# Another opening for a hybrid encoder block: value products in six PSUM banks, adaLN row sums in PSUM, norm sums on TensorE

## The chip, the cores and the metric

The kernel runs on one core of one Trainium2 chip, in one launch. Times are device microseconds of that core, from a profiled execution or from repeated timed runs; for repeated runs the median is given. TensorE (PE) multiplies matrices into PSUM, which has eight banks of 128 x 512 float32; VectorE (DVE), ScalarE (ACT) and GpSimd (POOL) work element by element; SyncE (SP) issues nearly all the DMA transfers.

## What is computed

One encoder block on 1024 positions of width 1024, float32, batch 1, conditioned by a vector `c`. Cut to what matters here:

```python
ada = silu(c) @ w_ada + b_ada                  # 6 x 1024 numbers
shift1, scale1, gate1, shift2, scale2, gate2 = split(ada, 6)
h = rmsnorm(x, g_mix) * (1 + scale1) + shift1
qa, ka, va, qb, kb, vb, ga, gb = split(h @ w_in)      # 8 heads of 64 in each branch; ga, gb are 1024 wide
oa = mixture_of_dilations(qa, ka, va, rel_bias)       # three banded softmaxes, merged by their denominators
ob = neighbourhood_attention_2d(qb, kb, vb, na_rpb)
x += gate1 * ((sigmoid(ga) * (oa @ w_branch_dil) + sigmoid(gb) * (ob @ w_branch_na)) @ w_out)
h2 = rmsnorm(x, g_ffn) * (1 + scale2) + shift2
u_val, u_gate = split(depthwise_conv3(h2 @ w_up))
x += gate2 * ((gelu(u_gate) * u_val) @ w_down)
y = rmsnorm(x, g_final)
```

## The kernel before

Positions lie on the free axis in two halves of 512 (`hf` = 0, 1); the width 1024 is cut into eight slices of 128 (`k`). Every large product is done three times in a reduced float32 format, "hi x hi, hi x lo, lo x hi", from operands split into a rounded part and the rest: `split` (L55, L56) makes the rounded part on ACT (`whi`, or `a`, `b` for value weights) and the rest on POOL (`wlo`). `h[hf, k]` holds such a pair for the modulated input.

The **opening** ends with the value projections written to DRAM. It is written in an order by hand (`tc.manual_schedule`): each engine and SP's DMA queue take their instructions in the order of the code, and what they wait for follows from the data and from the reuse of buffers. It consists of

- the norm: ACT squares `x` (L181), DVE adds the squares of four slices (L183), `norm_sums` sums over partitions on TensorE by one-column matmuls against `ones` (`add_sums`, L89), `rstd_of` (L94 to L96) makes the factor, and four transposes (`bcast`, L102) spread it over a bank `pbc`;
- the adaLN vector: `w_ada` comes in 12 chunks of 512 columns. For each, `ada_rows` multiplies eight rows by the numbers of `silu(c)` and adds them up on DVE in an SBUF tile `mt` (L149 for the first row, L151 for the rest), `ada_sums` sums over partitions on TensorE (L140), a bias is added (L167). The columns of chunks 0 to 3 are permuted so that each gives shift and scale of two slices `k` (`piece_bias`, L215 and L217);
- `modulate`: per slice DVE multiplies `x` by scale and norm into a PSUM tile `st` (L201, two buffers), ACT adds the shift and rounds to hi (L202), DVE makes lo (L204);
- the value products of two branches and two halves: `v_products` (L236 to L238), four banks of 128 positions, eight slices, three matmuls, 384 of 128x512 in all. They go as four sections of 96: branch 0 half 0 (as the pieces of adaLN become ready), branch 1 half 0, branch 0 half 1, branch 1 half 1. `v_out` (L246) copies four banks by ACT and stores them; banks come from a pool of five named `pj`;
- `warm` (L210): matmuls without a use, in front of the first products;
- loads of the first two query/key weights (`w_load`, L60), DRAM copies of the values in other orders (`va_chunks`, L252 and L254; `vb_chunks`, L456).

Behind the opening a scheduler orders the instructions: eight pairs of heads, each with query/key products (`qk_tiles`, which calls `product`, L77 to L79) and attention. A head of branch A takes its biases by DMA (L485, L486), adds `lnm` (loaded at L694) on POOL, and loads its values (`va_load`, L431 to L434); scores and softmax are L497 and L498, the transposes of P L520. Gates, branch products, output, and the ConvFFN follow.

Of the kernel before, what the change touches and what calls it, by code (L numbers as in the profile page):

```python
# [28 lines left out]
def hybrid_encoder(tc, xT, c, w_ada, small, w_in, w_v, p1_bias, p23_bias, na_bias, ln2_mult, ident, w_br, w_out,  # L29
# [101 lines left out]
    def stage():  # L131
        return ps.tile([128, 512], FT, name="st", bufs=2)

    def ada_sums(parts, pa=None, stop=True):

        first = pa is None
        pa = stage() if first else pa
        for i, (w, col) in enumerate(parts):
            for m in range(4):
                pe.matmul(pa[:, m:m + 1], w[:, m * 128:(m + 1) * 128], col, start=first and i + m == 0,  # L140
                          stop=stop and i == len(parts) - 1 and m == 3, skip_group_check=True)
        return pa

    def ada_rows(rows, ts, acc=None):

        for t in ts:
            if acc is None:
                acc = small_tile()
                dve.tensor_scalar(acc, rows[t], cs[:, t:t + 1], None, OP.mult)  # L149
            else:  # L150
                dve.scalar_tensor_tensor(acc, rows[t], cs[:, t:t + 1], acc, OP.mult, OP.add)  # L151
        return acc
# [12 lines left out]
    def ada_bias(c0, pa):  # L165
        cc = slice(c0, c0 + 4)
        dve.tensor_tensor(ada[:, cc], pa[:, :4], b_ada[:, cc], OP.add)  # L167

# [8 lines left out]
    def squares(x, engines):  # L177
        accs = []
        for k in range(KT):
            sq = small_tile()  # L180
            act.activation(sq, x[k], AF.Square)  # L181
            if k % 4:
                engines[k // 4].tensor_tensor(accs[-1], accs[-1], sq, OP.add)  # L183
            else:
                accs.append(sq)
        return accs

    def norm_sums(accs):
        pcol = ps.tile([128, 512], FT, name="pc")
        add_sums(pcol, accs[0], True, False)  # L190
        add_sums(pcol, accs[1], False, True)
        return pcol

    def modulate(x, hf, ks, pb):

        last = ()
        for k in [*ks, None]:
            if k is not None:
                hi, lo = h[hf, k] = h_tile(), h_tile()
                t, b = stage(), ada[:, k:k + 1]  # L200
                dve.scalar_tensor_tensor(t, x[k], am1[:, k:k + 1], pb, OP.mult, OP.mult)  # L201
                act.activation(hi, t, AF.Identity, bias=b)  # L202
            if last:
                dve.scalar_tensor_tensor(*last, OP.add, OP.subtract)  # L204
            last = k is not None and (lo, t, b, f(hi))
# [13 lines left out]
    v_raws = itertools.count()  # L219

    def v_load(br, kp):
        raw = wpool.tile([128, 2, 512], FT, name="wraw") if next(v_raws) % 4 < 2 else \
            early.tile([128, 2, 512], FT, name="vraw", bufs=2)
        sp.dma_start(raw, w_v[br, kp])
        return raw

    def v_split(raw, w, kp):
        for i in range(2):
            split(raw[:, i], w[0][:, 2 * kp + i], w[1][:, 2 * kp + i], pool)

    def v_products(w, hf, k, banks, ts=range(4)):
        hi, lo = w
        for t in ts:
            p = banks[t]
            hhi, hlo = (x[:, t * 128:t * 128 + 128] for x in h[hf, k])
            pe.matmul(p, hhi, hi[:, k], start=k == 0, stop=False, skip_group_check=True)  # L236
            pe.matmul(p, hhi, lo[:, k], start=False, stop=False, skip_group_check=True)
            pe.matmul(p, hlo, hi[:, k], start=False, stop=k == KT - 1, skip_group_check=True)  # L238

    def v_banks():  # L240
        return [ps.tile([128, 512], FT, name="pj", bufs=5) for _ in range(4)]

    def v_out(br, hf, banks):
        for t, p in enumerate(banks):
# [14 lines left out]
    pas = {}  # L259
    with tc.manual_schedule(engines={e.engine for e in (sp, act, dve, pool, pe)}):  # L260
        x = [x_load(0)]
        sp.dma_start(sm, small)
        rows = {0: ada_load(0, "t0")}
        raws = [v_load(0, 0)]
        rows[1] = ada_load(1, "b1")
        raws.append(v_load(0, 1))
        rows[2] = ada_load(2, "b2")
        raws += [v_load(0, kp) for kp in (2, 3)]
        rows[3] = ada_load(3, "t0")
        x.append(x_load(1))  # L270
        vw = [(t16("a0"), t16("a1"))]

        idle = ps.tile([128, 512], FT, name="pj", bufs=5)[:, :128]
# [9 lines left out]
        v_split(raws[0], vw[0], 0)  # L283
        pa = ada_sums([(acc, ones)])
        warm(6)
        banks = v_banks()
        for q in range(4):
            piece_bias(q, pa)
            modulate(x[0], 0, range(2 * q, 2 * q + 2), pb)
            v_products(vw[0], 0, 2 * q, banks)  # L290
            if q < 3:
                v_split(raws[q + 1], vw[0], q + 1)
                acc = ada_rows(rows[q + 1], range(6))
                pa = ada_sums([(rows[q + 1][t], cs[:, t:t + 1]) for t in (6, 7)], stop=False)
            else:
                accs = squares(x[1], (dve, dve))
            v_products(vw[0], 0, 2 * q + 1, banks, (0, 1))
            if q < 3:
                ada_sums([(acc, ones)], pa)
            v_products(vw[0], 0, 2 * q + 1, banks, (2, 3))  # L300
        raws = [v_load(1, kp) for kp in range(4)]
        vw.append((t16("b1"), t16("b2")))
        rows = {4: ada_load(4, "t0"), 5: ada_load(5, None)}
        pcol = norm_sums(accs)
        r = rstd_of(pcol, 4)
        for kp in range(2):
            v_split(raws[kp], vw[1], kp)
        qk_raw = []
        old = (0, 0, banks)
        accs = {}  # L310
        for n in range(24):
            g, k = divmod(n, 8)
            br, hf = ((1, 0), (0, 1), (1, 1))[g]
            if k == 0:
                v_out(*old)
                banks = v_banks()
                old = br, hf, banks
            if n == 17:
                va_chunks(slice(0, 512))
            v_products(vw[br], hf, k, banks)  # L320
            if n == 0:
                pb = bcast(r, ps, "pc")
                for kp in (2, 3):
                    v_split(raws[kp], vw[1], kp)
                modulate(x[1], 1, range(8), pb)
            if n in (5, 6):
                qk_raw.append(w_load(w_in[4 * (n - 5)]))
            i = n // 2 - 2
            if n % 2 == 0 and 0 <= i < 8:
                accs[i] = ada_rows(rows[4 + i], range(KT))  # L330
                if i < 6:
                    rows[6 + i] = ada_load(6 + i, (None, "t0")[i % 2 == 0])
            if n % 2 and n >= 9:
                i = (n - 9) // 2
                ada_bias(4 * (i + 4), ada_sums([(accs[i], ones)]))
            if n == 12:
# [996 lines left out]
```

## Time and profile before

| what | number |
|---|---|
| runs | 1573.51, 1574.42, 1581.34 us, median 1574.42 us |
| the profiled execution's own time | 1572.37 us |
| its span, first to last instruction | 1570.5 us |
| mean granted TensorE clock | 0.982 of full |
| PE busy | 1505.5 us (96%) |
| DVE, ACT, POOL busy | 1035.6, 779.1, 740.6 us |
| first value product, first query/key product | at 22.99 us, at 149.30 us |

In a row of the timeline stand the start, the duration, the engine, the line, the operation, what it writes and reads, and how many instructions the row groups; in square brackets the time for which the engine was idle before it, and what ended that. A matmul of 128x512 lasts longer than the distance to the next, because matmuls overlap: what counts is the distance of starts. A one-column matmul and a warming matmul show as two records each. In a row of windows the start and end come first, then the length, busy time and records of each engine, then the granted clock.

### The profile page before, as it was taken

How to read it: one execution, taken by the hardware profiler on the slowest of the kernel's cores; microseconds unless marked ns; L12 is line 12 of the kernel's file. 1: busy time of each engine (PE TensorE's matmuls, PEld its weight loads, DVE VectorE, ACT ScalarE, POOL GpSimd, SP SyncE). 2: the span in 40 equal slices, each digit the busy share in tenths (PEclk: the TensorE clock that was granted, in tenths of full speed). 3: DMA queues.
4: the chain of work that ended last, by engine and by line, in shares of the span. 5: the costliest groups of instructions: out<-in, count | busy, mean ns of one | idle time of the engine just before them, and what ended most of it. 6: DMA issues, size and time to landing. Idle time of an engine off the chain costs nothing.

```text
span 1570.5 us, 21187 instructions
## 1 busy us (share of the span) xinstructions
PE 1505.5 (96%) x7582; PEld 1267.3 (81%) x7582; DVE 1035.6 (66%) x1873; ACT 779.1 (50%) x1419; POOL 740.6 (47%) x475
## 2 busy tenths in 40 slices
PE   7998899999999999999999888999999999999998
PEld 6787788888888998887778777888888887778777
DVE  7694366576766655535534898776666667877765
ACT  3420466566765766643344454444444446575542
POOL 2310523233324444311145858676666665778621
PEclk8899999999999999999999999999999999999999
DMA  9577632323245565555544212322222224523313
GB/s 374 193 272 282 171 80 93 100 73 107 75 108 144 149 160 139 170 174 172 175 136 141 94 54 81 108 81 81 82 87 87 81 74 144 189 97 122 115 53 108
DMA packets 110001, 205.21 MB, mean 131 GB/s; under 512 B 40356, under 2 KB 55588, under 8 KB 109860
## 3 DMA queue, kind: packets, MB, share of 16 engines
q1 hardware_dynamic: 109624, 203.59, 40.3%
q8 instruction: 60, 0.98, 0.3%
q14 instruction: 45, 0.37, 0.1%
q10 hardware_dynamic: 272, 0.26, 0.1%
HBM read 158.73 MB, written 42.47 MB: 128 GB/s over the span
## 4 chain that ended last, share of the span: by engine, by line
PE 64%; DVE 12%; DMA 8%; POOL 6%; issue 4%; ACT 4%; SPq 1%; DVEq 0%; ACTq 0%; POOLq 0%
PE pj L822 8%; PE pj L823 8%; PE pj L824 8%; PE pj L79 8%; PE pj L77 8%; PE pj L78 8%; DMA g<-gs 2%; DMA wraw<-w_down 2%; PE pj L378 2%; DVE mt L151 2%; DVE big L1018 2%; PE O L672 2%; POOL wsl L56 2%; POOL wlo L56 1%; PE T L660 1%
## 5 line engine op out<-in xcount | busy, mean ns | idle before, releaser
L56 POOL TENSOR_TENSOR wlo<-wraw,whi 128x1024 fp32r<-128x1024 f32 (+1 forms) x77 | 178.9, 2323 | 249.6 <-ACT whi L55 224.4
L79 PE MATMUL pj<-h,wlo 128*128 128x512 f32 x448 | 178.6, 399 | 1.4 <-POOL wlo L56 1.4
L77 PE MATMUL pj<-h,whi 128*128 128x512 f32 x448 | 178.4, 398 | 0.1
L78 PE MATMUL pj<-h,whi 128*128 128x512 f32 x448 | 178.2, 398 | 0.0
L56 POOL TENSOR_TENSOR wsl<-big,wsh 128x1024 fp32r<-128x1024 f32 (+1 forms) x45 | 109.5, 2434 | 48.1 <-ACT wsh L55 48.0
L1018 DVE SCALAR_TENSOR_TENSOR big<-wc,sm,big 128x256 f32<-128x256 f32 (+1 forms) x132 | 116.8, 933 | 17.3 <-ACT big L1012 17.2
L55 ACT ACTIVATE whi<-wraw 128x1024 fp32r<-128x1024 f32 (+1 forms) x79 | 80.7, 1022 | 73.7 <-PE pj L78 30.0
L79 PEld LDWEIGHTS pj<-h,wlo 128*128 128x128 f32 x448 | 84.4, 188 | 16.3 <-POOL wlo L56 1.8
L78 PEld LDWEIGHTS pj<-h,whi 128*128 128x128 f32 x448 | 84.3, 188 | 14.4
L77 PEld LDWEIGHTS pj<-h,whi 128*128 128x128 f32 x448 | 84.4, 188 | 14.2 <-PE pj L79 0.5
L449 POOL TENSOR_TENSOR vv<-vv 96x256 fp32r<-96x256 f32 (+2 forms) x32 | 41.2, 1297 | 102.6 <-ACT vv L448 93.1
L498 ACT ACTIVATE P<-P,st 128x256 f32<-128x256 f32 x128 | 64.3, 503 | 49.6 <-DVE st L497 49.3
L385 POOL TENSOR_SCALAR qb<-qs 128x256 fp32r<-128x256 f32 x32 | 26.4, 851 | 124.0 <-PE S L544 57.9
L497 DVE CUSTOM_DVE_ANT_0 P<-S,bias 128x256 f32<-128x256 f32 x128 | 52.4, 421 | 42.3 <-PE S L544 23.2
L1018 DVE SCALAR_TENSOR_TENSOR big<-pj,sm,big 128x512 f32<-128x512 f32 x132 | 67.9, 565 | 16.1 <-ACT big L1012 16.1
L1012 ACT ACTIVATE big<-wc,sm 128x512 f32<-128x512 f32 x44 | 35.8, 816 | 75.7 <-DVE wc L835 45.3
L56 POOL TENSOR_TENSOR wsl<-wraw,wsh 128x768 fp32r<-128x768 f32 (+1 forms) x23 | 49.9, 2171 | 45.5 <-ACT wsh L55 45.5
L650 POOL TENSOR_SCALAR P<-P,stb 128x288 f32<-128x288 f32 (+1 forms) x32 | 39.9, 1248 | 66.0 <-DVE stb L647 58.8
L55 ACT ACTIVATE wsh<-big 128x1024 fp32r<-128x1024 f32 (+1 forms) x45 | 44.8, 1000 | 37.1 <-POOL big L787 23.6
L1044 ACT ACTIVATE big<-big 128x1024 f32<-128x1024 f32 x22 | 23.3, 1060 | 80.2 <-DVE big L1018 80.2
L503 DVE TENSOR_TENSOR tl<-T,th 128x512 fp32r<-128x512 f32 x64 | 43.7, 688 | 23.9 <-ACT th L502 23.5
L840 DVE TENSOR_TENSOR pj<-pj,wc 128x512 f32<-128x512 f32 x34 | 23.7, 696 | 47.0 <-PE pj L824 46.9
(366 smaller groups left out, 4862.3 us busy)
## 6 DMA issues: line engine op xcount, KB each, us to landing
wraw<-w_in SPq DMA_DIRECT2D x32, 512.0 KB, 4.2
t<-w_ada SPq DMA_DIRECT2D x24, 512.0 KB, 8.0
big<-w_up SPq DMA_DIRECT2D x22, 512.0 KB, 5.9
wraw<-w_up SPq DMA_DIRECT2D x22, 512.0 KB, 3.5
as<-big SPq DMA_DIRECT2D x22, 512.0 KB, 2.6
big<-as SPq DMA_DIRECT2D x22, 512.0 KB, 6.2
wraw<-w_down SPq DMA_DIRECT2D x24, 384.0 KB, 3.7
x<-w_ada SPq DMA_DIRECT2D x16, 512.0 KB, 9.9
```

Source lines behind the costliest of these rows:

```text
L55: act.activation(hi, raw, AF.Copy)
L56: lo_eng.tensor_tensor(lo, raw, f(hi), OP.subtract)
L77: pe.matmul(psum, whi[:, k0 + k], mhi, start=k == 0, stop=False)
L78: pe.matmul(psum, whi[:, k0 + k], mlo, start=False, stop=False)
L79: pe.matmul(psum, wlo[:, k0 + k], mhi, start=False, stop=k == n - 1)
L497: dve.tensor_tensor_reduce(pp, d, bias, -1.0, BIG, OP.add, OP.min, mi)
L498: act.activation(pp, pp, AF.Exp, bias=mi, scale=-1.0, accum_out=li)
L503: dve.tensor_tensor(tl, pt, f(th), OP.subtract)
L822: pe.matmul(psum, whi[:, k], bhi, start=j < 4 and k == 0, stop=False, skip_group_check=True)
L823: pe.matmul(psum, whi[:, k], blo, start=False, stop=False, skip_group_check=True)
L824: pe.matmul(psum, wlo[:, k], bhi, start=False, stop=k == n - 1, skip_group_check=True)
L1018: dve.scalar_tensor_tensor(y[:, dst], src, wt, y[:, dst], OP.mult, OP.add)
```

## The change

- **Norm of half 0.** Each of the eight squares is summed on TensorE at once; the adds on DVE go. `warm(3)` follows each pair.
- **First chunk.** All eight rows of `w_ada` chunk 0 are summed directly on TensorE (`ada_direct`), four before the transposes and four behind; `warm(8)` goes.
- **Six banks.** In the first section each slice `k` is multiplied for four banks of branch 0 and two of branch 1 (18 matmuls instead of 12). The next section has the two other banks of branch 1, then half 1 follows for branch 0 and branch 1. PSUM tiles are now eight named banks `b0` to `b7`.
- **Row sums.** `ada_rows` adds up in PSUM bank 6; of the pieces 1, 2 and 3 the first 4, 7 and 8 rows go this way and the rest directly to TensorE. Chunks 5 and 8 are scaled on ACT and added on POOL (`ada_scaled`). The squares of half 1 are added on POOL.
- **Modulation.** `normed` multiplies `x` by the norm in place (DVE); `modulated` does scale and shift on ACT into bank 7, a second ACT instruction rounds to hi, DVE makes lo.
- **Loads.** The value weights of both branches come interleaved with chunks 0 to 3, which use two tiles instead of three; `w_in`'s first loads move behind chunks 8 and 9.
- **Head inputs.** `lnm`, biases and values of heads 0 and 1 are issued ahead of the first `qk_tiles`; `vb_chunks` stands after the third pair of heads in the code instead of after the first.
- `dynamic_dma_scratch_size=64` is set for the program.

```diff
-    def ada_rows(rows, ts, acc=None):
-        for t in ts:
-            if acc is None:
-                acc = small_tile()
-                dve.tensor_scalar(acc, rows[t], cs[:, t:t + 1], None, OP.mult)
+    def ada_direct(rows, ts, pa, start=True, stop=True):
+        return ada_sums([(rows[t], cs[:, t:t + 1]) for t in ts], pa, start, stop)
+
+    def ada_rows(rows, n=KT):
+        acc, out = bank(6), small_tile()
+        for t in range(n):
+            dst = out if t == n - 1 else acc
+            if t == 0:
+                dve.tensor_scalar(dst, rows[t], cs[:, t:t + 1], None, OP.mult)
             else:
-                dve.scalar_tensor_tensor(acc, rows[t], cs[:, t:t + 1], acc, OP.mult, OP.add)
-        return acc
+                dve.scalar_tensor_tensor(dst, rows[t], cs[:, t:t + 1], acc, OP.mult, OP.add)
+            yield out
+
+    def ada_scaled(rows):
+        for t in range(KT):
+            act.activation(rows[t], rows[t], AF.Copy, scale=cs[:, t:t + 1])
+            if t:
+                pool.tensor_tensor(rows[0], rows[0], rows[t], OP.add)
+            yield rows[0]
...
+    def normed(x, k, pb):
+        dve.tensor_tensor(x[k], x[k], pb, OP.mult)
+
+    def modulated(x, hf, k):
+        hi, lo = h[hf, k] = h_tile(), h_tile()
+        t = bank(7)
+        act.activation(t, x[k], AF.Identity, bias=ada[:, k:k + 1], scale=am1[:, k:k + 1])
+        act.activation(hi, t, AF.Copy)
+        return lambda: dve.tensor_tensor(lo, t, f(hi), OP.subtract)
...
         warm(12)
-        accs = squares(x[0], (dve, dve))
-        pcol = norm_sums(accs)
-        acc = ada_rows(rows[0], range(3))
+        pcol = bank(7)
+        for k in range(KT):
+            sq = small_tile()
+            act.activation(sq, x[0][k], AF.Square)
+            add_sums(pcol, sq, k == 0, k == KT - 1)
+            if k % 2:
+                warm(3)
         r = rstd_of(pcol, 4)
-        warm(3)
-        pb = bcast(r, ps, "pc")
-        acc = ada_rows(rows[0], range(3, 8), acc)
-        warm(8)
+        pa = ada_direct(rows[0], range(4), bank(5), True, False)
+        pb = ps.tile([128, 512], FT, name="pbc", tag="b6")
...
+        ada_direct(rows[0], range(4, 8), pa, False, True)
...
         for q in range(4):
-            piece_bias(q, pa)
-            modulate(x[0], 0, range(2 * q, 2 * q + 2), pb)
-            v_products(vw[0], 0, 2 * q, banks)
+            k = 2 * q
+            v_products(0, 0, k, banks[0])
+            v_products(1, 0, k, banks[1], range(2))
             if q < 3:
...
+                n = (4, 7, 8)[q]
+                pa = bank(7)
+                acc = through(ada_rows(rows[q + 1], n))
+                if n < KT:
+                    ada_direct(rows[q + 1], range(n, KT), pa, True, False)
+                ada_sums([(acc, ones)], pa, n == KT)
...
+                piece_bias(q + 1, pa)
...
+                for i in range(2):
+                    modulated(x[0], 0, k + 2 + i)()
+            v_products(0, 0, k + 1, banks[0])
+            v_products(1, 0, k + 1, banks[1], range(2))
...
+        for k in range(KT):
+            v_products(1, 0, k, banks, (2, 3))
...
+            if k == 3:
+                pb = ps.tile([128, 512], FT, name="pbc", tag="b2")
...
+            if k >= 4:
+                second(k - 4)
+        second(4)
+        old = [(1, 0, banks)]
+        banks = {t: bank(2 + t) for t in range(4)}
+        for k in range(KT):
+            if k == 1:
+                v_out(*old.pop())
+            if k in (4, 5):
+                ada_chunk(k + 1, ended[k + 1], k - 4)
+            v_products(0, 1, k, banks)
+            if k < 5:
+                second(k + 5)
+            if k == 2:
+                rows[8] = ada_load(8, None)
+                rows[9] = ada_load(9, "t1")
+                qk_raw = [w_load(w_in[4 * i]) for i in range(2)]
+                rows[10] = ada_load(10, "t0")
...
+            if k == 5:
+                qk_w = [w_split(qk_raw[i], pool) for i in range(2)]
+            if k == 6:
+                ended[8] = through(ada_scaled(rows[8]))
+                ended[9] = through(ada_rows(rows[9]))
+        old = 0, 1, banks
+        banks = {t: bank(t) for t in range(4)}
+        for k in range(KT):
             if k == 0:
                 v_out(*old)
...
+    early_inputs = [dil_inputs(head) for head in range(2)]
+    qk = qk_tiles(0, 0, qk_w)
```

`second(k)` issues, for slice `k` of half 1, `normed` on DVE, the low part of the slice two before together with one row of chunk 6, and `modulated` of the slice before together with one scaled row of chunk 5.

How the order of instructions moves is shown at three places. On TensorE, from the first sums of the norm to the first value product; before:

```order
L89 MATMUL pc<-ones,mt 128x1 x8
L210 MATMUL pj<-idt 128x128 x3
L102 MATMUL pbc<-idt,rs 128x128 x4
L210 MATMUL pj<-idt 128x128 x8
L140 MATMUL st<-ones,mt 128x1 x4
L210 MATMUL pj<-idt 128x128 x6
L236 MATMUL pj<-a_148,h 128x512
```

After, from the last of the four pairs of squares:

```order
L89 MATMUL b_191<-ones,mt 128x1 x8
L209 MATMUL b_178<-idt 128x128 x3
L138 MATMUL b_256<-cs,t_112 128x1 x16
L279 MATMUL pbc<-idt,rs 128x128 x4
L138 MATMUL b_256<-cs,t_112 128x1 x16
L209 MATMUL b_178<-idt 128x128 x6
L233 MATMUL b_308<-a_174,h 128x512
```

The sums of one column stand at L89 and L138 now, the transposes at L279; between the last squares and the first product there are 32 one-column matmuls in place of four, and six warming matmuls directly ahead of the first product as before.

On DVE, where half 1 is modulated (`pbc` is the spread norm, `st` and `h` the modulated input; the number behind a name tells one buffer from another); before:

```order
L96 RECIPROCAL rs_520<-rs_520 128x4
L201 SCALAR_TENSOR_TENSOR st_575<-whi_140,am1_71,pbc_560 128x512
L201 SCALAR_TENSOR_TENSOR st_580<-whi_140,am1_71,pbc_560 128x512
L204 SCALAR_TENSOR_TENSOR h_574<-st_575,ada_70,h_573 128x512
L201 SCALAR_TENSOR_TENSOR st_586<-wlo_142,am1_71,pbc_560 128x512
L204 SCALAR_TENSOR_TENSOR h_579<-st_580,ada_70,h_578 128x512
L201 SCALAR_TENSOR_TENSOR st_592<-wlo_142,am1_71,pbc_560 128x512
L204 SCALAR_TENSOR_TENSOR h_585<-st_586,ada_70,h_584 128x512
```

After:

```order
L196 TENSOR_TENSOR whi_148<-whi_148,pbc_699 128x512 x2
L196 TENSOR_TENSOR wlo_150<-wlo_150,pbc_699 128x512
L204 TENSOR_TENSOR h_725<-b7_726,h_724 128x512
L151 TENSOR_SCALAR b6_738<-t1_169,cs_66 128x512
L196 TENSOR_TENSOR wlo_150<-wlo_150,pbc_699 128x512
L204 TENSOR_TENSOR h_742<-b7_743,h_741 128x512
L153 SCALAR_TENSOR_TENSOR b6_738<-t1_169,cs_66,b6_738 128x512
L196 TENSOR_TENSOR whi_152<-whi_152,pbc_699 128x512
L204 TENSOR_TENSOR h_758<-b7_759,h_757 128x512
L153 SCALAR_TENSOR_TENSOR b6_738<-t1_169,cs_66,b6_738 128x512
```

The multiplications by the norm (L196) now read and write `x` in place, and rows of chunk 6 (L153, in bank 6) stand between them. On TensorE the products of branch 0 half 1 begin in this place in bank 2, which held `pbc_699`; after:

```order
L233 MATMUL b1_661<-b1_176,h_546 128x512
L234 MATMUL b1_661<-b1_176,h_547 128x512
L235 MATMUL b1_661<-b2_177,h_546 128x512
L233 MATMUL b2_774<-a0_174,h_724 128x512
L234 MATMUL b2_774<-a0_174,h_725 128x512
L235 MATMUL b2_774<-a1_175,h_724 128x512
```

Before, they began in the one of the five banks `pj` that was free, and the next three came free by `v_out`.

On ACT, around the first copies of finished banks of half 1; before:

```order
L246 ACTIVATE mt<-pj 128x512 x4
L55 ACTIVATE b_496<-vraw 128x512 x4
L202 ACTIVATE h<-st,ada 128x512 x8
L246 ACTIVATE mt<-pj 128x512 x4
L55 ACTIVATE whi<-wraw 128x1024 x2
L246 ACTIVATE mt<-pj 128x512 x8
L368 ACTIVATE qs<-pj 64x512 x2
```

After (`b_774` is the first bank of branch 0 half 1):

```order
L202 ACTIVATE b_888<-wlo,ada,am_71 128x512
L203 ACTIVATE h<-b_888 128x512
L159 ACTIVATE x<-x,cs 128x512
L55 ACTIVATE whi<-wraw 128x1024 x2
L159 ACTIVATE x<-x,cs 128x512 x8
L240 ACTIVATE mt<-b_774 128x512
L240 ACTIVATE mt<-b_775 128x512
```

The two splits of `w_in` (L55) and eight scaled rows of chunk 8 (L159) now stand directly ahead of the copies of that section. On SP the loads behind which those splits wait stand like this; after:

```order
L177 DMA x<-w_ada 128x1024 x2
L177 DMA t_858<-w_ada 128x1024 x4
L60 DMA wraw<-w_in 128x1024 x2
L177 DMA t_867<-w_ada 128x1024 x4
L60 DMA wraw<-w_in 128x1024 x2
L241 DMA vas<-mt 128x512 x4
```

Before, where `t_678` is chunk 6:

```order
L162 DMA x<-w_ada 128x1024 x4
L247 DMA vas<-mt 128x512 x4
L162 DMA t_678<-w_ada 128x1024 x4
L60 DMA wraw<-w_in 128x1024 x2
L162 DMA x<-w_ada 128x1024 x4
```

`w_in`'s loads have moved from behind chunk 6 to behind chunks 8 (`x`) and 9 (`t_858`).

More of the change, by code (lines that the diff above doesn't have):

```diff
@@ new lines, in hybrid_encoder, with second @@
+            v_products(0, 0, k + 1, banks[0])
+            v_products(1, 0, k + 1, banks[1], range(2))
+        v_out(0, 0, banks[0])
+        v_out(1, 0, banks[1])
+        acc = through(ada_rows(rows[4]))
+        rows[7] = ada_load(7, "t0")
+        banks = {t: bank(t - 2) for t in (2, 3)}
+        scaled, summed = ada_scaled(rows[5]), ada_rows(rows[6])
+        lows = []
+        qk_raw = []
+        def second(k):
+            if k < KT:
+                normed(x[1], k, pb)
+            if k > 1:
+                lows.pop(0)()
+                ended[6] = next(summed)
+            if 0 < k <= KT:
+                lows.append(modulated(x[1], 1, k - 1))
+                ended[5] = next(scaled)
@@ L326, in hybrid_encoder @@
[L326 to L336, printed above, removed]
-                qk_w = [w_split(qk_raw[i], pool) for i in range(2)]
```

182 lines of the change are left out of this document (84 added, 98 removed).

## The prediction

> **What bounds the kernel now.** I read the page's span, engine shares and chain of waits first, then TensorE's timeline through the opening, then the windows.
>
> ```profile
> span 1570.5 us, 21187 instructions
> PE 1505.5 (96%) x7582; PEld 1267.3 (81%) x7582; DVE 1035.6 (66%) x1873; ACT 779.1 (50%) x1419; POOL 740.6 (47%) x475
> PE 64%; DVE 12%; DMA 8%; POOL 6%; issue 4%; ACT 4%; SPq 1%; DVEq 0%; ACTq 0%; POOLq 0%
> ```
>
> TensorE is busy for 96% and carries 64% of the chain, VectorE the next 12%, so little can be gained outside the opening, which ends where the first query/key product starts (L77):
>
> ```profile
> 22.99 0.50 PE L236 MATMUL pj<-a,h 128*128 128x512 f32 x1 [0.52 <-ACT h L202]
> 138.83 1.68 PE L140 MATMUL st<-ones,mt 128*128 128x1 f32 x8 [5.15 <-DVE ada L167]
> 148.49 0.95 PE L140 MATMUL st<-ones,mt 128*128 128x1 f32 x8
> 149.30 0.48 PE L77 MATMUL pj<-h,whi 128*128 128x512 f32 x1
> 71.11 0.39 PE L237 MATMUL pj<-b,h 128*128 128x512 f32 x1
> 78.36 0.39 PE L236 MATMUL pj<-b,h 128*128 128x512 f32 x1
> ```
>
> Products start every 0.227 us (71.11 and 78.36 are 32 products apart), so the 384 value products need 87.2 of the 126.3 us between 22.99 and 149.30. The rest is one-column sums, waits, and a clock that is not always full. The windows (PE busy and records, PEld, DVE, ACT, POOL, then the granted clock, DMA share and GB/s) show how it falls:
>
> ```profile
> 12.71:16.12 3.41, 3.39 (x16) 3.39 (x17) 3.03 (x7) 0.47 (x2) 0.00 (x0) 0.50 1.03 413
> 16.12:19.54 3.42, 3.42 (x18) 3.42 (x17) 3.31 (x4) 1.15 (x2) 1.64 (x2) 0.50 1.03 411
> 26.36:29.77 3.41, 3.17 (x21) 2.55 (x21) 3.30 (x4) 0.00 (x0) 0.65 (x1) 1.00 1.03 412
> 60.50:63.91 3.41, 2.41 (x20) 2.20 (x18) 1.05 (x4) 0.77 (x3) 0.00 (x0) 1.00 1.03 406
> 63.91:67.33 3.42, 2.85 (x6) 1.92 (x7) 0.00 (x0) 3.42 (x8) 3.38 (x3) 0.50 0.35 141
> 139.00:145.64 6.64, 6.64 (x21) 5.48 (x21) 5.62 (x11) 0.00 (x0) 0.00 (x0) 0.50 0.86 346
> ```
>
> The clock is granted in stretches of 3.41 us by what the stretch before did. 12.71 to 16.12 had TensorE busy without a pause, half of it on one-column sums, and yet the next stretch stayed at half. 60.50 to 63.91 was busy for 2.41 us, most of it such sums, and the clock fell. 26.36 to 29.77 held 1.5 us of such sums (the row of 26.18, below) and 55% products, and the clock stayed. I read from this that one-column sums count for almost nothing, and that some 45 to 55% of real streaming is needed.
>
> **The change, part by part.** The prices of TensorE's pieces:
>
> ```profile
> 2.75 4.42 PE L210 MATMUL pj<-idt 128*128 128x128 f32 x24 [2.75 <-DMA idt<-ident]
> 12.73 1.86 PE L89 MATMUL pc<-ones,mt 128*128 128x1 f32 x8 [1.99 <-DVE mt L183]
> 14.46 1.63 PE L210 MATMUL pj<-idt 128*128 128x128 f32 x6
> 15.88 1.06 PE L102 MATMUL pbc<-idt,rs 128*128 128x128 f32 x4
> 16.73 3.29 PE L210 MATMUL pj<-idt 128*128 128x128 f32 x16
> 20.89 1.58 PE L210 MATMUL pj<-idt 128*128 128x128 f32 x12
> 26.18 1.84 PE L140 MATMUL st<-cs,b 128*128 128x1 f32 x16
> ```
>
> Four one-column sums cost 0.81 us at the full clock (148.49 to 149.30), 1.73 at half (12.73 to 14.46). A warming record costs 0.13 (1.58/12) or 0.205 (3.29/16), two records to a warming matmul.
>
> *Until the first product.* DVE's adds of squares and of the first chunk go; TensorE gets thirteen more groups of four sums: eight instead of two for the squares, eight rows of the chunk instead of one sum. At the full clock: warm 12 ends at 7.2; four pairs of 2x0.81, three of them followed by warm 3 (0.8), end at 16.1; warm 0.8, four rows 3.24, transposes 0.7 (an estimate from 1.06 at half), four rows 3.24 reach 24.1; bias and modulation as before (20.89 to 22.99, 2.1) give 26.2, that is 3.2 later. But the stretches there hold 0.8 of warming in each 2.4 us, a third, below what held. So I take half clock from about 12.0, after two pairs: 2x3.46+1.2 for the others, then 1.2+6.9+1.06+6.9, then warm 6 at 2.5, give 38.7, that is 15.7 later. The next products still run a stretch or two at half, losing 3.4.
>
> *First section* (both branches, six banks, 144 products). 144x0.227 is 32.7; eight groups of row sums 6.5. The rows below price VectorE and ScalarE:
>
> ```profile
> 33.76 1.41 DVE L204 SCALAR_TENSOR_TENSOR h<-st,ada,h 128x512 fp32r<-128x512 f32 x2
> 71.07 1.42 DVE L201 SCALAR_TENSOR_TENSOR st<-whi,am,pbc 128x512 f32<-128x512 f32 x2 [7.51 <-PE pbc L102]
> 68.91 5.00 POOL L56 TENSOR_TENSOR b<-vraw,b 128x512 fp32r<-128x512 f32 x4
> 88.69 0.48 DVE L149 TENSOR_SCALAR mt<-x,cs 128x512 f32<-128x512 f32 x1
> 89.20 5.48 DVE L151 SCALAR_TENSOR_TENSOR mt<-x,cs,mt 128x512 f32<-128x512 f32 x7
> 96.88 9.55 DVE L151 SCALAR_TENSOR_TENSOR mt<-t,cs,mt 128x512 f32<-128x512 f32 x7
> 71.86 1.35 ACT L202 ACTIVATE h<-st,ada 128x512 fp32r<-128x512 f32 x2 [2.42 <-DVE st L201]
> 17.19 1.15 ACT L55 ACTIVATE a<-wraw 128x512 fp32r<-128x512 f32 x2 [2.16 <-DMA wraw<-w_v]
> ```
>
> No row shows an accumulator in PSUM. Nearest is L201, with a PSUM operand: 0.71, no slower while POOL ran (68.91). Bounds per step are 0.48 (88.69) and 0.79 (89.20); 1.36 (96.88, beside POOL) would be a loss beyond these. I take 0.79 for a row, 0.70 for the multiply and the low part. A piece then lasts: 7 or 8 rows 5.5 or 6.3, sum 0.8, bias 0.36, two modulations chained through bank 7 at 2.2 (0.69, 0.57, 0.70, hand-overs) 4.4: 11.1 and 11.9, against TensorE's 36 products and its sums, 9.8 and 9.0. Waits 1.3 and 2.9, plus three hand-overs of 0.5 (22.99): 5.7. The first piece (four rows) hides. Section: 44.9.
>
> *Third value section and the broadcast.* 48 products 10.9, norm sums 1.6, transposes 0.7, chunk sum 0.8: 14.1. The squares' six adds are now POOL's, 7.5 at 1.25 (68.91), hidden by 36 products before them, 8.2; uncovered they would hold the norm sums, at k=1. The broadcast lies in bank 2 at 7.8 (24 products 5.5, plus 1.6 and 0.7).
>
> *Second half of branch 0.* Its first bank is that bank 2, so it waits until DVE has made the last of eight multiplies, between which stand five low parts and five rows: 5.6+3.5+4.0 and hand-overs 1.2, 14.3, ending 22.1 after the section's start: a wait of 8.0. With every step at 0.48 it is 3.5, at 0.79 it is 9.1. Behind it TensorE's whole queue stands, nothing else. Then 96 products and two sums: 23.4.
>
> *Second half of branch 1.* Two banks are free (1.4 us); the third waits for the copy of the section before (L246), which on ACT stands behind two splits of w_in and eight scalings of chunk 8:
>
> ```profile
> 97.97 1.06 ACT L55 ACTIVATE whi<-wraw 128x1024 fp32r<-128x1024 f32 x1 [7.20 <-DMA wraw<-w_in]
> 115.43 0.60 ACT L246 ACTIVATE mt<-pj 128x512 f32<-128x512 f32 x1 [0.83 <-PE st L140]
> wraw<-w_in SPq DMA_DIRECT2D x32, 512.0 KB, 4.2
> ```
>
> On SP those w_in loads stand behind a tile of chunk 8 that waits for chunk 5's sum, 11.8 into the section before, and behind chunk 9. At 412 GB/s 512 KB take 1.28: 11.8+6x1.28+4.2 is 23.7, then 2x1.06+8x0.57+0.6: the bank is free at 31.0, wanted at 24.8: 6.2 of wait. If the tile comes free at once the wait is nothing; if w_in's loads share with chunk 10's four it is 11. The rest, 90 products and five sums, takes 24.5.
>
> Each of the two waits is followed by half clock, as 5.15 of idle at 138.83 was (139.00 to 145.64, 6.64 us doing the work of 3.3): 2x3.3.
>
> Together from the first product: 44.9+14.1+8.0+23.4+1.4+6.2+24.5+6.6 = 129.1, before 126.3. What the six banks and the loads save on TensorE (idle before: 5.15 and smaller) is given back.
>
> *Early head inputs.* The waits they could remove stand here:
>
> ```profile
> 168.78 8.38 SPq L456 DMA_DIRECT2D vb<-vbc  x12
> 173.71 0.51 PE L79 MATMUL pj<-h,wlo 128*128 128x512 f32 x1 [1.36 <-POOL wlo L56]
> 181.57 1.65 SPq L60 DMA_DIRECT2D wraw<-w_in  x2
> 187.59 1.06 ACT L55 ACTIVATE whi<-wraw 128x1024 fp32r<-128x1024 f32 x1 [3.05 <-DMA wraw<-w_in]
> 189.67 1.39 PE L520 MATMUL T<-idt,P 128*128 128x128 f32 x6 [2.38 <-ACT P L498]
> ```
>
> ACT's exponentials before 189.67 stood behind a split whose load went out after 12 copies of vb. Without: 1.36+2.38 and an estimated 1.7 of half clock, 5.4 at most, nothing at least. I take 5.4, as the loads now stand ahead. The smaller DMA scratch, the order of a product's three matmuls and the interleaved loads of both branches I cost at nothing: the six loads of a piece, 7.7 at 1.28, end within VectorE's 11 us for the one before, though chunk 2 now takes chunk 0's tile and loads only after that chunk's sums; without that cover each piece waits for two tiles, 2.6.
>
> **Sum**, against this execution's 1572.37 (the median, 1574.42, lies 2.05 above it): 15.7 + 3.4 + (129.1 - 126.3) - 5.4 = +16.5, so 1589.
>
> [...]
>
> **Rivals.** (1) The clock holds until the first product, since a third of warming is enough or sums do count: 3.2+2.8-5.4 = +0.6, 1573 (1566 to 1580). Against it: 16.12 stayed at half after a stretch without idling. For it: no stretch with exactly this mix is in the trace. (2) On the other side: VectorE's steps on PSUM cost 0.48, and the clock holds. The wait for bank 2 falls by 4.5, the pieces' by 3.8, and its half clock shrinks: 0.6-4.5-3.8-1.6 = -9.3, 1563 (1553 to 1566). It decides from about 0.55 a step. Against it L201's 0.71; for it L149's 0.48. (3) The head inputs bring nothing, because w_in's loads wait behind them as they did behind vb: 1589+5.4 = 1594.
>
> **How the numbers follow.** My forecast 0.50 (own range 1580 to 1597), rival 1 0.22, rival 2 0.18, rival 3 0.10. The range 1562 to 1597 leaves out half of rival 2 and some of rival 3. Half a percent (7.9 us) is about what a measurement of this kernel can tell from none: faster 0.20 (rival 2 and a little of 1), same 0.22 (most of 1, the low end of mine), slower 0.58.
>
> **What would show it.** In the new profile: the clock at 0.50 over 13 to 40 us and the first product near 39 (right) or near 26 (rival 1); the first product of the second half of branch 0 released by DVE after some 8 us; a wait of 6 us at the third bank of the last section, released by ACT; no wait of over 1 us between the first query/key product and the first transposes of P. Wrong would make it above all a chip that counts one-column sums as work, and VectorE steps below 0.55.

## The result, and the profile after

The changed kernel takes 1597.43 us (median of four runs, 1590.30 to 1599.83) against 1575.59 for the kernel before, measured with it: ratio 1.0134, 95% interval 1.0113 to 1.0154. It is 22 us slower, where the prediction's sum had 16.5 slower, 1589, with 1562 to 1597 as the range: the median lies at the upper edge, 0.4 above it. The profiled execution took 1596.82.

The page of the changed kernel: span, engines, chain of waits.

```profile
span 1595.0 us, 21409 instructions
PE 1534.5 (96%) x7680; PEld 1291.7 (81%) x7680; DVE 1008.0 (63%) x1838; ACT 800.3 (50%) x1451; POOL 762.6 (48%) x495
PE 82%; DVE 9%; DMA 3%; ACT 3%; issue 2%; POOL 1%; SPq 0%; DVEq 0%; ACTq 0%; POOLq 0%
```

TensorE is busy for 96% as before, and the kernel is longer: a busy TensorE at half the clock, or with products that start further apart, looks the same here. Its timeline through the opening:

```profile
2.57 5.49 PE L209 MATMUL b<-idt 128*128 128x128 f32 x24 [2.57 <-DMA idt<-ident]
18.83 3.41 PE L89 MATMUL b<-ones,mt 128*128 128x1 f32 x16
23.53 6.83 PE L138 MATMUL b<-cs,t 128*128 128x1 f32 x32
31.10 6.82 PE L138 MATMUL b<-cs,t 128*128 128x1 f32 x32
37.79 2.91 PE L209 MATMUL b<-idt 128*128 128x128 f32 x12
40.84 0.76 PE L233 MATMUL b<-a,h 128*128 128x512 f32 x1
74.96 1.02 PE L138 MATMUL b<-ones,mt 128*128 128x1 f32 x8 [2.79 <-DVE mt L153]
111.68 0.77 PE L233 MATMUL b<-a,h 128*128 128x512 f32 x1 [7.47 <-DVE wlo L196]
145.38 0.79 PE L233 MATMUL b<-b,h 128*128 128x512 f32 x1 [6.96 <-ACT mt L240]
172.21 0.39 PE L77 MATMUL pj<-h,whi 128*128 128x512 f32 x1
```

The first product starts at 40.84 (22.99 before), the first query/key product at 172.21 (149.30 before). The sums ahead of it cost twice their price at the full clock: 6.83 us for four rows of four sums (32 records), where 0.81 for each four had been read. Two new waits stand where the prediction had put them, and end by what it had named. Windows of the changed kernel (start and end, length, busy time and records of PE, PEld, DVE, ACT, POOL, then granted clock, DMA share, GB/s):

```profile
9.31:12.72 3.41, 3.41 (x30) 3.41 (x30) 0.00 (x0) 2.92 (x4) 0.00 (x0) 0.91 1.02 414
12.72:16.13 3.41, 3.41 (x17) 3.41 (x18) 0.00 (x0) 0.00 (x0) 0.00 (x0) 0.50 1.03 412
36.61:40.03 3.42, 3.42 (x17) 3.42 (x17) 1.09 (x4) 1.38 (x2) 0.00 (x0) 0.50 0.27 75
43.44:46.86 3.42, 3.42 (x21) 2.93 (x19) 3.31 (x6) 1.68 (x4) 3.42 (x4) 1.00 0.98 327
1116.00:1216.00 100.00, 100.00 (x432) 80.97 (x431) 68.86 (x100) 42.86 (x52) 65.10 (x38) 1.00 0.25 85
```

TensorE does not pause from 9.31 to 40.0, and yet the clock is at 0.50 from 12.72 to 40.03; the first products run from 40.84 on, and the window from 43.44 on is at 1.00. The last row lies far behind the opening, in the up-projection, and was not in the prediction. Before, the like stretch was

```profile
1100.00:1200.00 100.00, 100.00 (x442) 82.61 (x441) 68.85 (x102) 42.90 (x53) 65.41 (x36) 1.00 0.25 85
```

The code there is the same; TensorE is busy throughout at the full clock in both; but 432 matmuls show in 100 us in place of 442. By milestones of the two traces, the changed kernel is 22.9 us later at its first query/key product (172.21 against 149.30), 18.0 later at its first attention output (210.0 against 192.0), 16.1 later where the up-projection begins (901.3 against 885.2) and 25.4 later at its last products (1350.8 against 1325.4). The opening and the heads thus lose 18, the stages between drift by 2, and the up-projection loses 9.3 that the prediction does not have.

### The profile page after: what moved, and what is told of

Its sections match the earlier page's. It is cut to its first block, busy times and chain, and to the rows that moved or that the text cites. A ratio compares the mean times of both kernels' runs of the same rounds, so it can differ in the third digit from the quotient of the medians.

```text
span 1595.0 us, 21409 instructions
## 1 busy us (share of the span) xinstructions
PE 1534.5 (96%) x7680; PEld 1291.7 (81%) x7680; DVE 1008.0 (63%) x1838; ACT 800.3 (50%) x1451; POOL 762.6 (48%) x495
## 4 chain that ended last, share of the span: by engine, by line
PE 82%; DVE 9%; DMA 3%; ACT 3%; issue 2%; POOL 1%; SPq 0%; DVEq 0%; ACTq 0%; POOLq 0%
PE pj L882 11%; PE pj L880 11%; PE pj L881 11%; PE pj L79 9%; PE pj L77 9%; PE pj L78 9%; PE pj L431 2%; DVE big L1076 2%; PE O L732 2%; PE b L138 2%; PE b L233 2%; PE b L235 1%; PE b L234 1%; PE T L720 1%; PE S L699 1%
## 5 line engine op out<-in xcount | busy, mean ns | idle before, releaser
L55 ACT ACTIVATE whi<-wraw 128x1024 fp32r<-128x1024 f32 (+1 forms) x79 | 80.7, 1022 | 83.7 <-PE pj L78 35.7
L1076 DVE SCALAR_TENSOR_TENSOR big<-wc,sm,big 128x256 f32<-128x256 f32 (+1 forms) x132 | 100.6, 809 | 17.3 <-ACT big L1070 17.2
L557 DVE CUSTOM_DVE_ANT_0 P<-S,bias 128x256 f32<-128x256 f32 x128 | 52.3, 421 | 43.6 <-PE S L604 25.4
L1076 DVE SCALAR_TENSOR_TENSOR big<-pj,sm,big 128x512 f32<-128x512 f32 x132 | 67.8, 563 | 16.1 <-ACT big L1070 16.1
L55 ACT ACTIVATE wsh<-big 128x1024 fp32r<-128x1024 f32 (+1 forms) x45 | 44.8, 1000 | 39.9 <-POOL big L845 21.0
L563 DVE TENSOR_TENSOR tl<-T,th 128x512 fp32r<-128x512 f32 x64 | 43.7, 688 | 24.3 <-ACT th L562 23.7
L898 DVE TENSOR_TENSOR pj<-pj,wc 128x512 f32<-128x512 f32 x34 | 23.7, 697 | 51.9 <-PE pj L882 51.7
```

The lines of the kernel that those rows point to most:

```text
L55: act.activation(hi, raw, AF.Copy)
L557: dve.tensor_tensor_reduce(pp, d, bias, -1.0, BIG, OP.add, OP.min, mi)
L563: dve.tensor_tensor(tl, pt, f(th), OP.subtract)
L1076: dve.scalar_tensor_tensor(y[:, dst], src, wt, y[:, dst], OP.mult, OP.add)
```

## The experiments

Medians below stand beside the kernel before as measured with each set of runs (1575.0, 1577.1 and 1575.5 us).

### The scratch alone, and with other sizes

```diff
-    nc = bacc.Bacc("TRN2", target_bir_lowering=False, num_devices=1)
+    nc = bacc.Bacc("TRN2", target_bir_lowering=False, num_devices=1, dynamic_dma_scratch_size=64)
```

That the setting moves tiles to other addresses is the author's assumption: no trace shows an address. The first run is the kernel before with this line.

> The kernel before with only dynamic_dma_scratch_size=64 set, nothing else changed. In the up-projection TensorE started 442 products in 100 us before and 432 after the change, with no wait in either and the full clock. Theory A (the setting moves the tiles to other SBUF addresses, and products from those start 2% further apart): 432 to 434 in 100 us, and the whole kernel 7 to 10 us slower, about 1583. Theory B (the execution or the chip differed): 442 in 100 us and no difference, within 3 us.

Measured: 1583.83 us, ratio 1.005 (1.003 to 1.007): 8.8 us slower with no instruction changed. The traces of the two have the same instructions in the same order on each of the four engines, and in the up-projection TensorE starts 432 products from 1050 to 1150 in place of 442. The second run is the changed kernel with 1024 in place of 64.

> [...] If the distance of products hangs on the address within 1024 bytes (theory A in its narrow form): 442 products in 100 us of the up-projection, 7 to 10 us less than the changed kernel, about 1589. If it hangs on something else in the layout or on the execution (theory B): 432, and the time of the changed kernel, 1597.

Measured: 1587.33, ratio to before 1.0087 (1.0059 to 1.0114): 10.1 less than the changed kernel, 7 by the two ratios. The window 1050 to 1150 of each, the scratch of 64 (kernel before) first, then 1024 (changed kernel):

```profile
1050.00:1150.00 100.00, 100.00 (x432) 80.84 (x432) 67.35 (x100) 42.02 (x51) 65.04 (x36) 1.00 0.23 79
```

```profile
1050.00:1150.00 100.00, 100.00 (x441) 82.60 (x440) 67.19 (x99) 44.04 (x53) 67.25 (x37) 1.00 0.25 85
```

The counts are those of theory A: 432 with 64 in either kernel, 441 with 1024; its cause, other addresses, is not shown. Three single executions of the kernel before try 512, 256 and 128.

> [...] If only the address within 512 bytes (or less) counts: 442 products in 100 us of the up-projection, as before. If 1024 is the unit: 432.

> [...] If products need addresses that are equal within 256 bytes or less: 442 in 100 us of the up-projection; if 512 is the unit: 432.

> The same with scratch 128: 442 products in 100 us if 128 bytes (or less) are the unit, 432 if the unit is 256 or more.

```diff
+    nc = bacc.Bacc("TRN2", target_bir_lowering=False, num_devices=1, dynamic_dma_scratch_size=512)   # then 256, 128
```

The same window with 512, 256 and 128:

```profile
1050.00:1150.00 100.00, 100.00 (x442) 82.57 (x441) 68.36 (x99) 44.09 (x54) 67.59 (x38) 1.00 0.28 95
```

```profile
1050.00:1150.00 100.00, 100.00 (x442) 82.59 (x441) 66.65 (x99) 42.80 (x52) 66.80 (x37) 1.00 0.27 89
```

```profile
1050.00:1150.00 100.00, 100.00 (x432) 80.71 (x431) 69.23 (x100) 42.12 (x51) 64.36 (x36) 1.00 0.23 79
```

The count is 442 with 512 and 256, 432 with 128 (1573.02, 1572.95 and 1587.54 us, one time each). So with 1024, 512 and 256 the products stand as without the setting (441 or 442 in 100 us), with 128 and 64 2% further apart (432). With 64 this does not hold for all products: neighbouring query/key products start 0.230 us apart on average with it and 0.231 without, those of the up-projection that read `x` 0.233 and 0.227; with 128 the query/key products take 0.234 (0.230 without, both from 149 to 225 us). What ties the distance to the setting is not shown.

### The clock ahead of the first product

Each sum there multiplies by 128 equal columns in place of one.

```diff
-            add_sums(pcol, sq, k == 0, k == KT - 1)
+            wide_sums(pcol, sq, ones, k == 0, k == KT - 1)
...
+    def wide_sums(out, w, col, first, last):
+        for m in range(4):
+            pe.matmul(out[:, 128 * m:128 * m + 128], w[:, m * 128:(m + 1) * 128], col.to_broadcast([128, 128]),
+                      start=first and m == 0, stop=last and m == 3, skip_group_check=True)
```

(and so for the eight rows of chunk 0)

> The changed kernel, but each one-column sum ahead of the first product (squares of half 0 and chunk 0) multiplies by 128 equal columns instead of one; one of the 128 result columns is used. Each costs TensorE a little more (0.26 against 0.20 us at the full clock), and nothing else moves. Theory (the clock counts streamed columns): the clock stays at 1.00 from 9 us on and the first product starts at 30 to 32 us in place of 40.8; the kernel gains 8 to 12 us. Rival (the clock fell for another reason, such as the float32 weight loads or the wait for the data): clock 0.50 as before, first product at 45 to 50, the kernel 5 to 8 us slower.

Measured: 1587.12 us, ratio to before 1.0069 (1.0044 to 1.0094), 10.3 less than the changed kernel. Its timeline and windows:

```profile
17.09 3.74 PE L189 MATMUL b<-cs,t 128*128 128x128 f32 x32
21.11 3.74 PE L189 MATMUL b<-cs,t 128*128 128x128 f32 x32
26.80 0.51 PE L241 MATMUL b<-a,h 128*128 128x512 f32 x1 [0.62 <-ACT h L211]
```

```profile
12.72:16.13 3.41, 3.41 (x33) 3.41 (x32) 0.00 (x0) 0.00 (x0) 0.00 (x0) 1.00 1.03 409
16.13:19.55 3.42, 3.42 (x33) 3.42 (x32) 0.34 (x2) 1.25 (x3) 1.93 (x2) 1.00 1.02 407
```

The same 32 sums (16 a half; two records each) now take 3.6 instead of 6.7 us a half, since the clock stays at 1.00, and the first product starts at 26.80 in place of 40.84 (37.68 at the earliest in the other executions with this opening). A sum with 128 columns costs little more than one with a single column: 0.89 for four at the full clock (3.57 from 21.11 to 24.68, 16 sums) against 0.81. The weights, the warming between and the data are the same; only the columns differ. So the clock went with the columns (1.00 with 128 of them, 0.50 with one), and the rival is out. Of the 14.0 us won at the first product 10.3 reach the end; the next row sums have one column again, and behind them products start 0.43 apart from 39.05 to 43.74, in place of 0.23.

### The wait for bank 2

```diff
-            if k < KT:
-                normed(x[1], k, pb)
...
+            if k == 4:
+                for i in range(KT):
+                    normed(x[1], i, pb)
             if k >= 4:
                 second(k - 4)
```

> The changed kernel, but in half 1 all eight multiplications by the norm stand together on DVE, ahead of the low parts and the rows of chunk 6. Theory (the last of these multiplications holds bank 2, and nothing else holds the second half of branch 0): the wait of 7.5 us before its first product falls to 0 to 2 us, with it the stretch at half clock behind it (1.7), and the kernel gains 6 to 9 us. Rival (the wait passes to the modulation, which begins 4 us later): the wait becomes 4 to 5 and the gain 2 to 3.

Measured: 1593.78 us, ratio to before 1.0121 (1.0098 to 1.0144): 3.7 less than the changed kernel, though the intervals of the two overlap. The wait of 7.47 is gone, a new one stands further on, and the wait for the copies, 6.96 in the changed kernel, is shorter:

```profile
121.39 1.87 PE L138 MATMUL b<-ones,x 128*128 128x1 f32 x8 [6.16 <-POOL x L161]
143.38 0.79 PE L233 MATMUL b<-b,h 128*128 128x512 f32 x1 [4.36 <-ACT mt L240]
```

The first row is the sum of chunk 5, whose rows are scaled on ACT one by one between the modulations and added on POOL. The section's products start 7.7 us earlier now (104.01 against 111.68), while POOL's adds end 2.5 later (121.33 against 118.83). That DVE's multiplications held the bank is shown; that nothing stood behind them was wrong. The two waits together fall from 14.4 to 10.5, which fits the 3.7. The rival named the modulation, with a wait of 4 to 5 and a gain of 2 to 3; what waited was this sum, for 6.16.

### The wait for the copies

```diff
-            if k == 5:
-                qk_w = [w_split(qk_raw[i], pool) for i in range(2)]
             if k == 6:
-                ended[8] = through(ada_scaled(rows[8]))
                 ended[9] = through(ada_rows(rows[9]))
...
                 v_out(*old)
...
+                ended[8] = through(ada_scaled(rows[8]))
+                qk_w = [w_split(qk_raw[i], pool) for i in range(2)]
```

> The changed kernel, but the copies of the finished banks of branch 0 half 1 stand on ACT ahead of the eight scalings of chunk 8 and the two splits of w_in; chunk 8's sum moves from the fourth to the sixth slice of the last section, the two behind it one slice on. Theory (those ten instructions hold the third bank of the last section): the wait of 7.0 us there goes, with it the half clock behind it, and the kernel gains 7 to 9 us against the changed kernel, about 1589. Rival (the work only moves: chunk 8's sum or the first query/key weights come too late): a new wait of 4 to 7 us at that sum or at the first L77, no gain.

Measured: 1587.60 us, ratio to before 1.0070 (1.0046 to 1.0095), 9.8 less than the changed kernel. No wait is left in the last section: from the first product of branch 0 half 1 to the first query/key product it takes 51.6 us in place of 60.5.

```profile
108.69 0.77 PE L233 MATMUL b<-a,h 128*128 128x512 f32 x1 [7.50 <-DVE wlo L196]
160.32 0.48 PE L77 MATMUL pj<-h,whi 128*128 128x512 f32 x1
```

### The early head inputs

```diff
-    early_inputs = [dil_inputs(head) for head in range(2)]
     qk = qk_tiles(0, 0, qk_w)
+    early_inputs = []
```

> The changed kernel, but the biases, lnm and values of heads 0 and 1 are issued behind the first query/key tiles again (heads 0 and 1 each where they are used). Theory (the early inputs took away the waits of 1.4 and 2.4 us): such waits are back behind the first L77 and the kernel is 4 to 6 us slower than the changed one. Rival (those waits went because the opening is longer and vb's copies had more time): no difference, within 2 us.

Measured: 1599.10 us, ratio to before 1.0130 (1.0105 to 1.0155), no difference from the changed kernel. The rival holds. The scheduler orders these instructions by itself, and the order on TensorE, and on the three other engines, is the same with and without the early statement. The second part of that edit alone, on the kernel before:

```diff
-            if n == 0:
+            if n == 2:
                 for hv in range(2):
                     vb_chunks(slice(hv * 256, hv * 256 + 256))
```

> The kernel before, with vb_chunks standing after the third pair of heads in the code, as in the changed kernel; nothing else. Theory (it is the copies of vb ahead of the head inputs that made the third w_in load and so the exponentials late): the waits of 1.4 and 2.4 us go, gain 4 to 6 us. Rival (the order of the queue hardly changes, and the waits went in the changed kernel because its opening is longer): no difference, within 2 us.

Measured: 1572.81 us, ratio to before 0.9983 (0.9966 to 1.0000): the medians differ by 2.7, between the two theories and not clear of the noise. The wait of 2.38 is gone, that of 1.36 stays, and a new one of 1.48 has come:

```profile
170.61 0.47 PE L77 MATMUL pj<-h,whi 128*128 128x512 f32 x1 [1.48 <-DVE qs L369]
172.64 0.50 PE L79 MATMUL pj<-h,wlo 128*128 128x512 f32 x1 [1.32 <-POOL wlo L56]
187.63 0.85 PE L520 MATMUL T<-idt,P 128*128 128x128 f32 x6
```

From the first query/key product (146.88) to the first attention output (189.38) 42.5 us pass, 42.7 before, so that nothing is won in the stretch that this edit was to shorten.

### All together

> All that the runs so far point to, in one kernel: the changed one with the norm's adds and chunk 0's rows on DVE again until the first product, scratch 1024, the eight multiplications by the norm of half 1 together, chunk 5 scaled and half of chunk 6's rows summed ahead of them, the sums of chunks 5 and 6 one slice earlier and later, w_in's loads ahead of chunk 9, and the copies ahead of chunk 8's scalings. If the waits add up as told: first product at 22 to 24, first query/key product at 128 to 136 in place of 172 (149 before the change), the up-projection as before the change, the kernel 1548 to 1560, 15 to 25 us faster than before the change. If TensorE waits elsewhere in place of those waits (rows of DVE, w_ada's loads): 1565 to 1580.

Its edits are the scratch of 1024, the norm first and the copies first, as in the runs above, with the squares and chunk 0 as before the change (added on DVE), `w_in`'s loads ahead of chunk 9's, the sums of the last section at slices 1, 3, 5, 6 and 7, and besides:

```diff
+        for _ in range(4):
+            next(summed)
...
                 r = rstd_of(pcol, 4)
+                ended[5] = through(scaled)
...
-            if k in (4, 5):
-                ada_chunk(k + 1, ended[k + 1], k - 4)
+            if k in (3, 6):
+                ada_chunk(k // 3 + 4, ended[k // 3 + 4], k // 3 - 1)
```

Measured: 1564.84 us, ratio to before 0.9927 (0.9905 to 0.9949). It beats both kernels: 12 us less than the one before, 33 less than the changed one. It misses the expected 1548 to 1560 by five and lies at the edge of the other case, in which TensorE waits elsewhere. The first query/key product starts at 133.76, as expected, but less than that comes out at the end:

```profile
133.76 0.48 PE L77 MATMUL pj<-h,whi 128*128 128x512 f32 x1
151.58 0.77 PE L77 MATMUL pj<-h,whi 128*128 128x512 f32 x1 [6.56 <-DVE qs L440]
```

```profile
149.04 1.06 ACT L519 ACTIVATE vv<-vv 128x1024 fp32r<-128x1024 f32 x1 [8.88 <-DMA vv<-vab]
```

Of 15.5 us won by then, 6.56 and a stretch at half clock are lost: ACT waits 8.88 us for the values of head 0, loaded late, ahead of the copies of queries that free TensorE's banks. The last run puts those copies first.

```diff
-    early_inputs = [dil_inputs(head) for head in range(2)]
-    qk = qk_tiles(0, 0, qk_w)
+    with tc.manual_schedule(engines={act.engine}):
+        qk = qk_tiles(0, 0, qk_w)
+        early_inputs = [dil_inputs(head) for head in range(2)]
```

> e8_best, with one thing more: during the first query/key tiles ACT takes its instructions in the order of the code, so that the copies of the values of heads 0 and 1 (which wait for a late load of vab) stand behind the copies of the first queries and keys instead of between them. Theory (that wait on ACT held TensorE for 6.6 us at 151 us and brought two stretches of half clock): the wait goes, the first scores start 6 to 10 us earlier, and the kernel gains 6 to 10 us against e8_best, about 1557. Rival (the loads behind, of w_in and vb, hold TensorE next): gain under 3.

Measured: 1566.27 us, ratio to before 0.9937 (0.9916 to 0.9958): no gain. The rival holds, a wait in place of a wait:

```profile
170.27 0.79 PE L592 MATMUL S<-ks,qs 128*128 128x256 f32 x2 [7.36 <-DMA ks<-ks]
```

On SP the copies of the keys (`ks<-ks`, out at 163.69) stand behind 16 copies of vb, out from 151.93 on. A shorter opening shows how much of the head inputs' loading it had hidden.

## Why the prediction came out as it did

**Until the first product: right, in size too.** 38.7 was forecast, 40.84 came; two thirds of the 2.1 that are missing are the first warming matmuls (5.49 against 4.42) and the six last at half clock (2.91 against 2.46). In the other traces with the same opening it came at 37.68 to 40.85, so a miss of this size is within what executions differ by. The cause, columns and not busy time, is shown by the run with 128 columns: the clock fell to 0.50 without a gap (3.41 of 3.41 us busy from 12.72 on), and held at 1.00 when the same gapless work had 128 columns. In the traces of the two kernels the granted clock is 1.00 or 0.50 and changes on a grid of 3.41 us (in the opening of the kernel before to half at 9.30, 43.44, 63.91 and 139.01, back at 19.54, 46.85, 70.74 and 145.83). The 45 to 55% of streaming in the prediction are the author's estimate from three stretches; no run tried shares around it.

**First section: the sum was close because two errors cancel.** 44.9 and 3.4 of half clock make 48.3; it lasted 49.0 (40.84 to 89.89, where the next section's first product starts). Of the 5.7 of waits in the sum only 2.79 came: the second piece did not wait, and the three hand-overs do not show. Half clock cost about 6 instead of 3.4, since the clock fell twice more, behind the sums of the first piece and behind the third one's wait: products start 0.43 apart from 51.6 to 56.3 and from 77.2 to 80.1.

```profile
50.23:53.64 3.41, 3.41 (x11) 2.92 (x11) 0.87 (x3) 1.38 (x2) 0.00 (x0) 0.50 0.91 304
```

DVE's price of a row with the sum in PSUM was the open one:

```profile
69.32 4.71 DVE L153 SCALAR_TENSOR_TENSOR b<-t,cs,b 128x512 f32<-128x512 f32 x6
110.85 0.68 DVE L196 TENSOR_TENSOR wlo<-wlo,pbc 128x512 f32<-128x512 f32 x1
```

0.785 a row (4.71/6), and 0.68 for the multiplication, against 0.79 and 0.70 taken. The rival of 0.48 is out. The 2.79 is the third piece's wait, 2.9 by the sum.

**The two banks.** 7.47 where 8.0 stood, by DVE's last multiplication; 6.96 where 6.2 stood, by ACT's copy:

```profile
137.61 1.06 ACT L55 ACTIVATE whi<-wraw 128x1024 fp32r<-128x1024 f32 x1 [20.21 <-DMA wraw<-w_in]
138.89 1.06 ACT L55 ACTIVATE whi<-wraw 128x1024 fp32r<-128x1024 f32 x1 [0.22 <-DMA wraw<-w_in]
139.85 4.99 ACT L159 ACTIVATE x<-x,cs 128x512 f32<-128x512 f32 x8
144.75 2.01 ACT L240 ACTIVATE mt<-b 128x512 f32<-128x512 f32 x4
```

The ten instructions are there in a row. The first split came 25.9 us after the section's start, 23.7 by the sum. Of half clock behind the two waits about 3 us showed, not 6.6 (seven and eight products at about 0.43 instead of 0.229). From the first product to the first query/key product it took 131.4; the terms gave 132.5 with the 3.4.

**Early head inputs: the size was right by luck.** From the first query/key product to the first attention output 37.8 us passed, 42.7 before: 5.0 less, 5.4 by the term. But the early statement did nothing, and the later place of `vb_chunks` alone leaves 42.5. What this stretch goes with in the traces is how late the opening ends. It takes 47.6 and 46.6 in the two runs with all together, where the first query/key product starts at 133.8 and 135.2; 41.4 to 42.7 in the kernel before and three of its variants (146.9 to 149.3); 37.8 to 39.2 in the changed kernel and three of its variants (160.3 to 173.5). While TensorE is held up in the opening, SP goes on: the first values of head 0 go out 11.7 us behind the first query/key product in the kernel before, 2.4 in the changed one (first row before, second after).

```profile
160.99 0.43 SPq L431 DMA_DIRECT2D vv<-vas  x1
174.58 0.42 SPq L484 DMA_DIRECT2D vv<-vas  x1
```

So the longer opening most likely gave the loads their time. No run changes its length alone, so this cause is argued and not shown.

**The step that failed** is "The smaller DMA scratch, the order of a product's three matmuls and the interleaved loads of both branches I cost at nothing". The scratch alone costs 8.8 us on the kernel before and 10.1 (7 by the ratios) in the changed one; the two other parts were not tried alone. The profiled execution took 1596.82 where the sum gave 1588.9; with this one term, 8.8, the sum is 1597.7. That it comes so close is partly luck: until the first attention output 18.0 us are lost against the sum's 16.5, and the stages up to the up-projection then give 2 back. The prediction looked only where the change moves instructions; this part of it moves none.

## What to carry to other kernels

Price one-column matmuls by what they do to the clock as well as by their time: 64 of them, with little warming between, brought the first product 11 to 14 us later than the same 64 with 128 columns, which kept the full clock for 10% more each. A setting of the program belongs into the sum like an instruction, also where it changes none (the scratch of 64 cost 8.8 us): compare the count of matmuls in a long stretch without waits, before and after. When a wait is taken away by reordering, look at once at what stands next in each queue: the sum of chunk 5, the values' copy and the keys' copy each took over most of the wait before it.

## What the runs showed of the hardware that was not expected

- With a scratch of 64 or 128 TensorE started 432 products of the up-projection in 100 us in place of 442, at the same granted clock of 1.00 and without a wait (100.00 us busy); with 256 and 512 it started 442, with 1024 441. The query/key products were slower with 128 (0.234 us, 0.230 without, both from 149 to 225 us) but not with 64 (0.230, 0.231 without).
- A float32 sum with 128 columns cost 0.89 us for four, with one column 0.81: the 127 columns more came to 0.02 us a sum. The weight loads were busy throughout in both (3.41 of 3.41 us, from 9.31 with one column and from 12.72 with 128).
- DVE added into PSUM at 0.785 us a row of 128x512, the same as into SBUF while POOL was idle (0.78 by 5.48/7). Beside a busy POOL it was no slower (five rows in 3.92, first row, while POOL was busy for all of 57.10 to 60.51), unlike the rows in SBUF before (1.36 by 9.55/7, from 96.88 to 106.43, with POOL busy for 5.19 of these 9.55).

```profile
56.65 3.92 DVE L153 SCALAR_TENSOR_TENSOR b<-t,cs,b 128x512 f32<-128x512 f32 x5
57.10:60.51 3.41, 3.41 (x16) 2.79 (x15) 3.27 (x5) 0.20 (x1) 3.41 (x4) 1.00 1.03 411
```
